# A hybrid decoder layer: gate columns in one operand, a token-major output gate, shared PSUM banks and alternating matmul widths

## Chip, cores and metric

The kernel runs on one core of one Trainium2 chip. The time is the device time of one execution in microseconds; what is compared is the median over runs.

## The reference

One layer on 256 tokens of width 2048, in float32. A token mixer (a gated delta rule of 8 heads and a pooling branch of 4 groups) shares one input projection and one output projection; a cross-attention into 256 memory tokens and a squared-ReLU MLP of width 8192 follow. The lines that matter here:

```python
proj = h @ w_in[l]                       # columns: q, k, v (3W), z (W), b (H), a (H), p
o_gdn = gated_deltanet(qkv, z, b, a, conv_w[l], a_log[l], dt_bias[l], gdn_norm_w[l])
o_pool = multiscale_pool(p, pool_w[l], pool_scale[l])
mix = jnp.concatenate([o_gdn, o_pool], axis=-1) @ w_out[l]
h = layer_norm(DEEPNORM_ALPHA * h + mix, ln1_g[l], ln1_b[l])
xa = memory_cross_attention(h, mem, xq_w[l], xk_w[l], xv_w[l], xo_w[l])
h = layer_norm(DEEPNORM_ALPHA * h + xa, ln2_g[l], ln2_b[l])
ff = jnp.square(jax.nn.relu(h @ w_up[l])) @ w_down[l]
h = layer_norm(DEEPNORM_ALPHA * h + ff, ln3_g[l], ln3_b[l])

# inside gated_deltanet
beta = jax.nn.sigmoid(b)
g = -jnp.exp(a_log) * jax.nn.softplus(a + dt_bias)
o = chunk_gated_delta_rule(q, k, v, g, beta)
o = o * lax.rsqrt(jnp.mean(o * o, axis=-1, keepdims=True) + NORM_EPS) * norm_w
o = o * jax.nn.silu(z.reshape(shp))

# inside multiscale_pool, for each of the 4 groups of 256 channels
mixed = jnp.einsum("btgc,gcd->btgd", pooled, pool_w)
return mixed.reshape(bsz, t_len, POOL_WIDTH) * pool_scale
```

## The kernel before, in words

All large products run on TensorE in a split float32: `split` (L185) writes a rounded copy of a tensor (H, the high part, ScalarE at L189) and the rest (L, the low part, VectorE at L190), both as fp32r, and a product is high times high, high times low and low times high. Weights arrive as tiles of 256 rows by 512 columns (tag W, four buffers), are split into H and L (three buffers each), and are used once. `run` (L225) walks one plan of such tiles: for tile t it issues loads, emits the splits of tiles ahead, emits the matmuls of tile t, and then lets `bg.step` (L83) emit background work (the recurrence, norms, attention) up to a budget of VectorE and ScalarE time. This order of emission is the order in which each engine executes.

Two forms of projection exist. `proj_a` (L313) keeps weights stationary and gives feature-major results. In its wide form one tile takes 8 matmuls of 512 moving columns (H against the high and low halves of the activations side by side, L328) and 8 of 256 columns (L against the high half, L332); the narrow form uses three of 256 (L349). `proj_b` (L367) keeps activations stationary and gives token-major results: one tile takes 12 matmuls of 512 columns (L374 to L376), for each of two token blocks and two row blocks in turn.

Order of the plan: w_in[0], the gate projection (`gates_plan`, L627: two tiles of 128 padded columns, of which 16 are used), w_in[1] (narrow), w_in[2] to [9] (wide; 6 and 7 are z, 8 and 9 are p), w_k 0 to 2, `pool_map(0)` (L993), w_k 3, `pool_map(1)`, w_out, w_v, w_q, w_o, and four rounds of w_up and w_down. The gates' background work (`gates`, L649) transposes the gate columns into a PSUM tile and reads it. `z_evac` (L923) folds the two halves of a wide result on ScalarE and GpSimd, and `silu` applies SiLU later; `solve` (L837) ends the recurrence and scales its output per token (L916); `gate_out` (L938) transposes each head, multiplies by norm weight and silu(z) on VectorE, and splits the result for w_out.

`pool_map` makes one 256 by 256 product for each of two groups. Each half of 128 columns (`nb`) takes 6 matmuls of 256 columns (L1003 to L1005) into a PSUM tile of its own, after which ScalarE writes the high part (L1009) and VectorE the low part (L1010), both reading PSUM. PSUM has 8 tiles of 512 columns, one bank each: four under the tag acc, which rotate, and four under aux. Waits between engines are put in by the framework from the tiles that instructions touch.

Second layer norm: `Norm.start` of token block 1 stands behind the last tile of w_o, `Norm.turn` (L1304) transposes pairs of blocks between the first up-projection tiles, and `norm1.scale(1, ALL)` (L1110 through L1336) stands behind the third of these tiles. `beside` (L1112) does the other blocks on ScalarE and GpSimd.

Of the kernel before, what the change touches and what calls it, by code (L numbers as in the profile page):

```python
# [9 lines left out]
F32 = mybir.dt.float32  # L10
F32R = mybir.dt.float32r
# [4 lines left out]
P = 128  # L16
T = 256
# [107 lines left out]
def hybrid_layer(ctx: ExitStack, tc: tile.TileContext, xT, xtok, memT, w_ba, w_in, small, w_pool,  # L125
# [99 lines left out]
    def run():  # L225
# [24 lines left out]
        def do_split():  # L250
            i = pos["split"]
            kind, src, shape, fn = plan[i][:4]
            if kind in "fwh":
# [59 lines left out]
    def proj_a(src, acts, evac, kt_outer=False, load=None, fine=0, pre=None, wide=False, spread=False):  # L313
        accs = []

        def tile_fn(k0, ns):
            def fn(h, l):
# [8 lines left out]
                def first(s, n):  # L326
                    c = slice(n * P, (n + 1) * P)
                    mm(out=accs[n], lhsT=h[:, s, c], rhs=acts[k0 + s].wide, start=k0 + s == 0, stop=False)  # L328

                def second(s, n):  # L330
                    c = slice(n * P, (n + 1) * P)
                    mm(out=accs[n][:, :T], lhsT=l[:, s, c], rhs=acts[k0 + s][0], start=False, stop=k0 + s == KT - 1)  # L332

                if wide:

                    for part in ([[(s, n) for s in range(ns)] for n in range(4)] if last else [order]):
                        for s, n in part:
                            first(s, n)
                        for s, n in part:
                            second(s, n)  # L340
# [26 lines left out]
    def proj_b(src, acts, evac, resident=False, pre=None, post=None):  # L367
# [12 lines left out]
        def both(j):  # L380
            def fn(h, l):
                if j == 0:
                    accs.extend(acc() for _ in range(NT))
                for t in range(NT):
                    for s in range(2):
                        one(t, 2 * j + s, h[:, s, :], l[:, s, :])
# [57 lines left out]
    nc.gpsimd.memset(m64[0:64, 64:128], 1.0)  # L444
    eps_ln = const.tile([P, 1], F32, name="eps_ln")
# [181 lines left out]
    def gates_plan():  # L627
        pb = []

        def fn(j):  # L630
            def f(h, l):
                if j == 0:
                    pb.append(acc())
                o = pb[0][:, :T]
                for s in range(8):
                    kt = 8 * j + s
                    a = xs[kt]
                    mm(out=o, lhsT=h[:, s, :], rhs=a[0], start=kt == 0, stop=False)
                    mm(out=o, lhsT=h[:, s, :], rhs=a[1], start=False, stop=False)
                    mm(out=o, lhsT=l[:, s, :], rhs=a[0], start=False, stop=kt == KT - 1)  # L640
                if j == 1:
                    ba.append(chunk([T]))
                    S.activation(out=ba[0], in_=o, func=AF.Copy)
                    bg.event("ba")
            return f
# [935 lines left out]
```

## Time and profile before

| | us |
|---|---|
| median of 3 runs | 1483.5 (1483.07 to 1484.04) |
| the profiled execution, its own time | 1483.14 |
| its span in the trace | 1481.3 |
| TensorE matmuls busy | 1472.4 (99%) |
| VectorE busy | 943.4 (64%) |
| ScalarE busy | 728.2 (49%) |
| GpSimd busy | 148.8 (10%) |

The span is the time from the first to the last instruction of the program in the trace; the execution's own time has 1.8 us more around it. A matmul's end is modelled and overlaps the next one, so the cost of a matmul is read from the distance of two starts, not from its duration. A timeline row merges equal instructions that follow each other (xN), and what stands in square brackets is the engine's idle time before it and what ended it.

### The profile page before, as it was taken

What the parts mean: (1) busy time and instruction counts of PE and PEld (TensorE: products, weight loads), DVE (VectorE), ACT (ScalarE), POOL (GpSimd) and SP (SyncE); (2) the same over time, 40 slices, a digit from 0 to 9 for tenths busy, and PEclk for the clock granted to TensorE, in tenths of its full rate; (3) what the DMA queues carried; (4) which work ended last, traced back from release to release, by engine and by line L of the source; (5) the groups of instructions that cost most, each with busy time, mean ns of one, the idle gap of its engine ahead of it and who ended that gap; (6) DMA issues with size and microseconds to landing.
All of it is one profiled execution on the core that took longest, in us unless ns stands there. A gap on an engine that the chain in (4) does not pass through costs nothing.

```text
span 1481.3 us, 21143 instructions
## 1 busy us (share of the span) xinstructions
PE 1472.4 (99%) x8050; PEld 1277.3 (86%) x8050; DVE 943.4 (64%) x1464; ACT 728.2 (49%) x1064; POOL 148.8 (10%) x191
## 2 busy tenths in 40 slices
PE   9999999999999999999999999999999999999998
PEld 9988889899888888998888888888888888888887
DVE  6778976867656755555685555566545565556557
ACT  6765555755533545453545443355344453345442
POOL 1024323700300000000130000000000000000001
PEclk9999999999999999999999999999999999999999
DMA  8556565535865555444735655555656655555562
GB/s 274 182 203 185 171 187 173 194 130 170 288 197 189 183 190 190 155 133 159 276 131 178 199 191 190 196 187 183 198 190 212 222 192 194 196 190 185 194 233 83
DMA packets 86902, 280.45 MB, mean 189 GB/s; under 512 B 13920, under 2 KB 15216, under 8 KB 86800
## 3 DMA queue, kind: packets, MB, share of 16 engines
q1 hardware_dynamic: 79072, 268.73, 54.7%
q0 software_dynamic: 2960, 9.58, 2.0%
q10 hardware_dynamic: 4768, 0.79, 0.3%
q8 instruction: 63, 1.03, 0.3%
q14 instruction: 39, 0.32, 0.1%
HBM read 276.43 MB, written 2.63 MB: 188 GB/s over the span
## 4 chain that ended last, share of the span: by engine, by line
PE 98%; DVE 1%; ACT 0%; issue 0%; DMA 0%; DVEq 0%; ACTq 0%
PE acc L328 30%; PE acc L332 15%; PE acc L374 13%; PE acc L376 13%; PE acc L375 13%; PE acc L349 5%; PE acc L411 0%; PE acc L410 0%; PE acc L409 0%; PE acc L1377 0%; PE acc L1379 0%; PE acc L1378 0%; PE aux L1224 0%; PE aux L1223 0%; PE aux L855 0%
## 5 line engine op out<-in xcount | busy, mean ns | idle before, releaser
L190 DVE TENSOR_TENSOR L<-W,H 128x1024 fp32r<-128x1024 f32 x469 | 578.1, 1234 | 462.2 <-ACT H L189 456.6
L189 ACT ACTIVATE H<-W 128x1024 fp32r<-128x1024 f32 x479 | 507.4, 1059 | 582.7 <-PE acc L376 298.7
L328 PE MATMUL acc<-c,H 128*128 128x512 f32 x1920 | 499.2, 394 | 0.0
L328 PEld LDWEIGHTS acc<-c,H 128*128 128x128 f32 x1920 | 338.3, 189 | 55.3 <-DVE c L190 0.6
L374 PE MATMUL acc<-H,c 128*128 128x512 f32 x832 | 325.2, 391 | 0.0
L376 PE MATMUL acc<-H,c 128*128 128x512 f32 x832 | 323.9, 389 | 0.0
L375 PE MATMUL acc<-L,c 128*128 128x512 f32 x832 | 323.9, 389 | 0.0
L332 PEld LDWEIGHTS acc<-c,L 128*128 128x128 f32 x1920 | 274.2, 190 | 27.2
L332 PE MATMUL acc<-c,L 128*128 128x256 f32 x1920 | 281.3, 282 | 0.0
L376 PEld LDWEIGHTS acc<-H,c 128*128 128x128 f32 x832 | 156.2, 188 | 32.6
L375 PEld LDWEIGHTS acc<-L,c 128*128 128x128 f32 x832 | 156.3, 188 | 31.7
L374 PEld LDWEIGHTS acc<-H,c 128*128 128x128 f32 x832 | 156.2, 188 | 31.7
L204 POOL TENSOR_TENSOR c<-c 128x256 f32<-128x256 f32 x60 | 49.8, 855 | 369.9 <-DVE L L190 186.6
L190 DVE TENSOR_TENSOR c<-c,c 128x256 fp32r<-128x256 f32 (+1 forms) x170 | 76.6, 503 | 11.4 <-ACT c L189 11.4
L189 ACT ACTIVATE c<-c 128x256 fp32r<-128x256 f32 (+1 forms) x170 | 66.6, 456 | 4.6 <-DMA c<-xT 4.6
L349 PE MATMUL acc<-c,H 128*128 128x256 f32 x384 | 66.7, 290 | 0.7 <-ACT H L189 0.7
L1095 POOL DMA_DIRECT2D c<-lnrow x24 | 12.9, 539 | 517.8 <-PE acc L376 345.0
L349 PEld LDWEIGHTS acc<-c,H 128*128 128x128 f32 x384 | 58.2, 198 | 1.6 <-ACT H L189 1.4
L349 PE MATMUL acc<-c,L 128*128 128x256 f32 x192 | 48.0, 289 | 0.0
L201 ACT ACTIVATE c<-acc 128x512 f32<-128x512 f32 x60 | 35.6, 599 | 18.9 <-PE acc L332 14.9
L566 DVE SCALAR_TENSOR_TENSOR c<-c,par 128x255 f32<-128x255 f32 (+2 forms) x72 | 38.2, 538 | 3.6 <-ACT c L563 1.9
L349 PEld LDWEIGHTS acc<-c,L 128*128 128x128 f32 x192 | 34.4, 197 | 0.2 <-DVE L L190 0.2
(258 smaller groups left out, 1000.8 us busy)
## 6 DMA issues: line engine op xcount, KB each, us to landing
W<-w_up SPq DMA_DIRECT2D x127, 512.0 KB, 4.2
W<-w_down SPq DMA_DIRECT2D x120, 512.0 KB, 4.3
W<-w_in SPq DMA_DIRECT2D x76, 512.0 KB, 3.4
W<-w_k SPq DMA_DIRECT2D x32, 512.0 KB, 3.4
W<-w_out SPq DMA_DIRECT2D x32, 512.0 KB, 4.3
W<-w_v SPq DMA_DIRECT2D x32, 512.0 KB, 3.3
W<-w_q SPq DMA_DIRECT2D x32, 512.0 KB, 3.3
W<-w_o SPq DMA_DIRECT2D x24, 512.0 KB, 3.5
```

The source lines that it names most:

```text
L189: S.activation(out=h, in_=src, func=AF.Copy)
L190: eng.tensor_tensor(out=l, in0=src, in1=h.bitcast(F32), op=ALU.subtract)
L201: S.activation(out=ab.rearrange("p s c -> p (s c)"), in_=o, func=AF.Copy)
L204: nc.gpsimd.tensor_tensor(out=r, in0=ab[:, 0, :], in1=ab[:, 1, :], op=ALU.add)
L328: mm(out=accs[n], lhsT=h[:, s, c], rhs=acts[k0 + s].wide, start=k0 + s == 0, stop=False)
L332: mm(out=accs[n][:, :T], lhsT=l[:, s, c], rhs=acts[k0 + s][0], start=False, stop=k0 + s == KT - 1)
L349: mm(out=accs[n][:, :T], lhsT=w[:, s, n * P:(n + 1) * P], rhs=acts[kt][x], start=kt == 0 and w is h and x == 0, stop=kt == KT - 1 and w is l)
L374: mm(out=accs[t], lhsT=a[0][:, c], rhs=h, start=kt == 0, stop=False)
L375: mm(out=accs[t], lhsT=a[0][:, c], rhs=l, start=False, stop=False)
L376: mm(out=accs[t], lhsT=a[1][:, c], rhs=h, start=False, stop=kt == KT - 1)
L566: V.scalar_tensor_tensor(out=u[:, sh:], in0=x[:, :T - sh], scalar=w[:, 3 - sh:4 - sh], in1=u[:, sh:], op0=ALU.mult, op1=ALU.add)
L1095: nc.gpsimd.dma_start(out=c, in_=lnrow[i:i + 1, g * 512:(g + 1) * 512].partition_broadcast(P))
```

## The change

The gate projection gets 16 columns. One tile holds its high and low parts side by side (32 stationary columns), and 16 matmuls of 512 columns replace 48 of 256; four small fp32 products with a matrix of two stacked identities (`twos`) add the four partial sums and put tokens on partitions, where two transposes stood. z goes through `proj_b`: SiLU is applied straight from PSUM, `solve` multiplies by it while it scales, and `gate_out` writes the two parts of the result from the transposed head with one ScalarE and one VectorE operation. `proj_b` (without `resident`) goes through a tile by operand first (H with the high, H with the low, L with the high part of the activations) and by token block second. `pool_map` puts both halves of a group into one PSUM tile. `norm1.scale(1, ALL)` moves from behind the third up tile to directly behind `norm1.start`. In the query projections 0 to 2 and in 15 of the 16 up projections (`turn=True`) every other tile runs its 256-column matmuls first, so that equal widths meet at the border of two tiles.

```diff
@@ -250,7 +250,11 @@
         def do_split():
             i = pos["split"]
             kind, src, shape, fn = plan[i][:4]
-            if kind in "fwh":
+            if kind in "wh" and shape == [KT, 16]:
+                h = wp.tile([P, KT, 32], F32R, tag="H", name=nm("H"), bufs=HB)
+                split(h[:, :, 0:16], h[:, :, 16:32], raw.pop(i), KT * 16)
+                parts[i] = (h, None)
...
@@ -323,21 +329,25 @@
                 if wide and k0 == 0:
                     order = [i for i in order if i[1] < 3] + [i for i in order if i[1] == 3]
 
-                def first(s, n):
+                def first(s, n, ends):
                     c = slice(n * P, (n + 1) * P)
-                    mm(out=accs[n], lhsT=h[:, s, c], rhs=acts[k0 + s].wide, start=k0 + s == 0, stop=False)
-
-                def second(s, n):
+                    mm(out=accs[n], lhsT=h[:, s, c], rhs=acts[k0 + s].wide, start=k0 + s == 0,
+                       stop=ends and k0 + s == KT - 1)
+
+                def second(s, n, ends):
                     c = slice(n * P, (n + 1) * P)
-                    mm(out=accs[n][:, :T], lhsT=l[:, s, c], rhs=acts[k0 + s][0], start=False, stop=k0 + s == KT - 1)
+                    mm(out=accs[n][:, :T], lhsT=l[:, s, c], rhs=acts[k0 + s][0], start=False,
+                       stop=ends and k0 + s == KT - 1)
 
                 if wide:
 
+
                     for part in ([[(s, n) for s in range(ns)] for n in range(4)] if last else [order]):
-                        for s, n in part:
-                            first(s, n)
-                        for s, n in part:
-                            second(s, n)
+                        low = turn and width[0] == "low" and k0 > 0
+                        for step in (second, first) if low else (first, second):
+                            for s, n in part:
+                                step(s, n, step is (first if low else second))
+                        width[0] = "high" if low else "low"
...
@@ -381,9 +391,17 @@
             def fn(h, l):
                 if j == 0:
                     accs.extend(acc() for _ in range(NT))
-                for t in range(NT):
-                    for s in range(2):
-                        one(t, 2 * j + s, h[:, s, :], l[:, s, :])
+                last = 2 * j + 2 == KT
+
+                for ts in [[t] for t in range(NT)] if last else [range(NT)]:
+                    for x, w in ((0, h), (1, h), (0, l)):
+                        for t in ts:
+                            for s in range(2):
+                                kt = 2 * j + s
+                                mm(out=accs[t], lhsT=acts[kt][x][:, t * P:(t + 1) * P], rhs=w[:, s, :],
+                                   start=kt == 0 and x == 0 and w is h, stop=kt == KT - 1 and w is l)
+                    if last:
+                        evac(ts[0], accs[ts[0]])
...
+    twos = const.tile([P, 16], F32, name="twos")
+    V.tensor_tensor(out=twos, in0=ident[:, 0:16], in1=ident[:, 16:32], op=ALU.add)
...
@@ -625,26 +645,15 @@
     ba = []
 
     def gates_plan():
-        pb = []
-
-        def fn(j):
-            def f(h, l):
-                if j == 0:
-                    pb.append(acc())
-                o = pb[0][:, :T]
-                for s in range(8):
-                    kt = 8 * j + s
-                    a = xs[kt]
-                    mm(out=o, lhsT=h[:, s, :], rhs=a[0], start=kt == 0, stop=False)
-                    mm(out=o, lhsT=h[:, s, :], rhs=a[1], start=False, stop=False)
-                    mm(out=o, lhsT=l[:, s, :], rhs=a[0], start=False, stop=kt == KT - 1)
-                if j == 1:
-                    ba.append(chunk([T]))
-                    S.activation(out=ba[0], in_=o, func=AF.Copy)
-                    bg.event("ba")
-            return f
-        for j in range(2):
-            add("w", w_ba[j], [8, P], fn(j))
+        def fn(hl, _):
+
+            o = acc()
+            for kt in range(KT):
+                mm(out=o[0:32, :], lhsT=hl[:, kt, :], rhs=xs[kt].wide, start=kt == 0, stop=kt == KT - 1)
+            ba.append(chunk([2, T]))
+            S.activation(out=ba[0][0:32].rearrange("p s c -> p (s c)"), in_=o[0:32, :], func=AF.Copy)
+            bg.event("ba")
+        add("w", w_ba, [KT, 16], fn)
...
@@ -654,14 +663,16 @@
         yield from free_aux()
         pt = aux()
         for a in range(NT):
-            nc.tensor.transpose(out=pt[:, a * P:(a + 1) * P], in_=ba[0][:, a * P:(a + 1) * P], identity=ident)
+            for s in range(2):
+                mm(out=pt[:, a * 16:a * 16 + 16], lhsT=ba[0][0:32, s, a * P:(a + 1) * P], rhs=twos[0:32, :],
+                   start=s == 0, stop=s == 1)
...
@@ -911,45 +922,42 @@
         r = small_tile([NT, 4])
         rsqrt(r, ms, [NT, 4])
         yield 1.2, 1.5, 0
+        while f"z{g}" not in bg.done:
+            yield 0, 0, 1
         for a in range(NT):
             for i in range(4):
-                V.tensor_scalar(out=os_[a][:, i, :], in0=os_[a][:, i, :], scalar1=r[:, a, i:i + 1],
-                                scalar2=None, op0=ALU.mult)
-                yield .2, 0, 0
+                V.scalar_tensor_tensor(out=os_[a][:, i, :], in0=os_[a][:, i, :], scalar=r[:, a, i:i + 1],
+                                       in1=four(zsil[g][a])[:, i, :], op0=ALU.mult, op1=ALU.mult)
+                yield .22, 0, 0
         og[g] = os_
 
-    zsil = [None] * 4
+    zsil = [[None] * NT for _ in range(2)]
 
     def z_evac(g):
-        def evac(n, o):
-            h = 4 * g + n
-            if h % 2 == 0:
-                zsil[h // 2] = chunk([2, T])
-            bg.urgent.append(silu(h, fold(o, zsil[h // 2][:, h % 2, :])))
+
+        def evac(t, o):
+            zsil[g][t] = chunk([512])
+            S.activation(out=zsil[g][t], in_=o, func=AF.Silu)
+            bg.charge(0, .65)
+            if t == NT - 1:
+                bg.event(f"z{g}")
         return evac
 
-    def silu(h, z):
-        yield 0, 0, 1
-        yield 0, 0, 1
-        S.activation(out=z, in_=z, func=AF.Silu)
-        bg.event(f"z{h}")
-        yield 0, .35, 0
-
     def gate_out(h):
+
         g, n = h // 4, h % 4
-        zs = zsil[h // 2][:, h % 2, :]
         yield from free_aux()
         ps = aux()
         for a in range(NT):
             nc.tensor.transpose(out=ps[:, a * P:(a + 1) * P], in_=og[g][a][:, n, :], identity=ident)
         yield 0, 0, 1
-        V.scalar_tensor_tensor(out=zs, in0=ps[:, :T], scalar=par[:, C_NW:C_NW + 1], in1=zs,
-                               op0=ALU.mult, op1=ALU.mult)
+        mix[8 + h] = m = pair()
+        sc = par[:, C_NW:C_NW + 1]
+        S.activation(out=m[0], in_=ps[:, :T], func=AF.Copy, scale=sc)
+        V.scalar_tensor_tensor(out=m[1], in0=ps[:, :T], scalar=sc, in1=m[0].bitcast(F32), op0=ALU.mult,
+                               op1=ALU.subtract)
         done()
-        yield .4, 0, 1
-        mix[8 + h] = pair()
-        split(*mix[8 + h], zs)
-        yield .35, .3, 0
+        yield .5, .4, 0
...
@@ -994,9 +1002,9 @@
 
         def fn(h, l):
             for gi in range(2):
+                ps = acc()
                 for nb in range(2):
-                    ps = acc()
-                    o = ps[:, :T]
+                    o = ps[:, nb * T:(nb + 1) * T]
                     for s in range(2):
...
-    proj_a(w_in[6], xs, z_evac(0), wide=True)
-    proj_a(w_in[7], xs, z_evac(1), wide=True)
+    proj_b(w_in[6], xs, z_evac(0))
+    proj_b(w_in[7], xs, z_evac(1))
...
-        proj_a(w_q[g], f1, q_evac, wide=g < 3, kt_outer=g == 0, pre={0: ["ln1_0", "ln1_1"]} if g == 0 else None)
+        proj_a(w_q[g], f1, q_evac, wide=g < 3, turn=True, kt_outer=g == 0, pre={0: ["ln1_0", "ln1_1"]} if g == 0 else None)
...
-        15: steps((norm1.start, 5, [half0, half1, (1, ALL)], [half0, half1], (2, 3))),
+        15: steps((norm1.start, 5, [half0, half1, (1, ALL)], [half0, half1], (2, 3)), (norm1.scale, (1, ALL))),
     }
     after_up = {
-        2: steps((norm1.turn, 0, 1), (norm1.scale, (1, ALL))),
+        2: steps((norm1.turn, 0, 1)),
...
-            proj_a(w_up[4 * qd + g], f2, u_evac, wide=True, spread=True)
+            proj_a(w_up[4 * qd + g], f2, u_evac, wide=True, spread=True, turn=True)
...
-        "w_ba": wba.reshape(2, 8, P, P).transpose(0, 2, 1, 3),
+        "w_ba": wba.reshape(KT, P, 16).transpose(1, 0, 2),
```

## Rows read from the trace of the kernel before

**Rows 1.** The page: busy time of each engine, granted clock in slices.

```profile
PE 1472.4 (99%) x8050; PEld 1277.3 (86%) x8050; DVE 943.4 (64%) x1464; ACT 728.2 (49%) x1064; POOL 148.8 (10%) x191
...
PEclk9999999999999999999999999999999999999999
```

**Rows 2.** Waits of PE: line, waited for, total us, times, longest.

```profile
PE aux L1311 <- DVE c L1110: 0.7, 1, 0.7
```

**Rows 3.** Timeline of PE, wide up projection: start us, us, engine, line.

```profile
963.41 0.40 PE L328 MATMUL acc<-c,H 128*128 128x512 f32 x1
...
969.00 2.00 PE L328 MATMUL acc<-c,H 128*128 128x512 f32 x8
...
971.79 2.00 PE L328 MATMUL acc<-c,H 128*128 128x512 f32 x8
...
985.75 0.63 PE L328 MATMUL acc<-c,H 128*128 128x512 f32 x2
```

**Rows 4.** Timeline of PE, from before to after four down projections.

```profile
1030.43 0.40 PE L374 MATMUL acc<-H,c 128*128 128x512 f32 x1
...
1117.49 0.39 PE L328 MATMUL acc<-c,H 128*128 128x512 f32 x1
```

**Rows 5.** Timeline of PE around gate projection and gate products.

```profile
30.56 0.28 PE L638 MATMUL acc<-c,H 128*128 128x256 f32 x1
...
36.32 0.40 PE L349 MATMUL acc<-c,H 128*128 128x256 f32 x2
...
39.20 0.38 PE L657 MATMUL aux<-ident,c 128*128 128x128 f32 x2
39.34 0.48 PE L349 MATMUL acc<-c,H 128*128 128x256 f32 x2
...
57.02 0.29 PE L700 MATMUL aux<-t,upper 128*128 128x16 f32 x2
57.15 0.37 PE L701 MATMUL aux<-t,ones 128*128 128x16 f32 x2
```

**Rows 6.** Timeline of PE and DVE at the second layer norm.

```profile
769.27 0.44 PE L1311 MATMUL aux<-ident,c 128*128 128x128 f32 x2 [0.75 <-DVE c L1110]
...
764.93 0.15 DVE L1121 SCALAR_TENSOR_TENSOR t<-t,t 128x1 f32<-128x1 f32 x1
...
767.79 1.42 DVE L1110 SCALAR_TENSOR_TENSOR c<-c,t,c 128x512 f32<-128x512 f32 x1
```

**Rows 7.** Timeline of DVE and ACT, two readers of one PSUM tile.

```profile
63.81 0.18 DVE L705 COPY G<-aux 128x32 f32<-128x32 f32 x1
...
64.03 0.27 ACT L710 ACTIVATE c<-aux 16x128 f32<-16x128 f32 x1 [1.39 <-DVE G L705]
```

**Rows 8.** Timeline around both calls of pool_map (PE, ACT, DVE).

```profile
347.83 0.28 PE L1003 MATMUL acc<-c,H 128*128 128x256 f32 x1
...
347.80 0.59 ACT L896 ACTIVATE c<-aux 128x512 f32<-128x512 f32 x1
...
349.23 1.57 ACT L1009 ACTIVATE c<-acc,par 128x256 fp32r<-128x256 f32 x4
...
350.51 1.65 DVE L1010 SCALAR_TENSOR_TENSOR c<-acc,par,c 128x256 fp32r<-128x256 f32 x4
...
375.06 0.28 PE L1003 MATMUL acc<-c,H 128*128 128x256 f32 x1
...
377.57 1.65 DVE L1010 SCALAR_TENSOR_TENSOR c<-acc,par,c 128x256 fp32r<-128x256 f32 x4
```

**Rows 9.** Evacuations of pool_map by line: ns min/median/max, first and last start.

```profile
L1009 ACT ACTIVATE c<-acc,par x8: 468/482/503, 349.2 to 377.4; 128x256 fp32r<-128x256 f32 x8
...
L1010 DVE SCALAR_TENSOR_TENSOR c<-acc,par,c x8: 473/474/478, 350.5 to 378.7; 128x256 fp32r<-128x256 f32 x8
```

**Rows 10.** Busy time by stretch: us, PE to POOL (instructions), granted clock, DMA.

```profile
5.00:10.40 5.40, 5.26 (x24) 5.26 (x25) 3.71 (x8) 3.23 (x8) 0.00 (x0) 1.00 0.95 321
10.40:36.00 25.60, 25.60 (x216) 25.60 (x215) 17.82 (x29) 17.40 (x31) 0.00 (x0) 1.00 0.86 288
```

More of the change, by code (lines that the diff above doesn't have):

```diff
@@ L252, in do_split @@
             kind, src, shape, fn = plan[i][:4]
-            if kind in "fwh":
+            if kind in "wh" and shape == [KT, 16]:
+                h = wp.tile([P, KT, 32], F32R, tag="H", name=nm("H"), bufs=HB)
+                split(h[:, :, 0:16], h[:, :, 16:32], raw.pop(i), KT * 16)
+                parts[i] = (h, None)
+            elif kind in "fwh":
                 h = wp.tile([P] + shape, F32R, tag="H", name=nm("H"), bufs=HB)
@@ L310, in add, with proj_a @@
         plan.append((kind, src, shape, fn, pre, post))
-    def proj_a(src, acts, evac, kt_outer=False, load=None, fine=0, pre=None, wide=False, spread=False):
+    width = ["low"]
+    def proj_a(src, acts, evac, kt_outer=False, load=None, fine=0, pre=None, wide=False, spread=False, turn=False):
         accs = []
@@ L656, in gates @@
         for a in range(NT):
-            nc.tensor.transpose(out=pt[:, a * P:(a + 1) * P], in_=ba[0][:, a * P:(a + 1) * P], identity=ident)
+            for s in range(2):
+                mm(out=pt[:, a * 16:a * 16 + 16], lhsT=ba[0][0:32, s, a * P:(a + 1) * P], rhs=twos[0:32, :],
+                   start=s == 0, stop=s == 1)
         yield 0, .2, 1
-        ptv = pt[:, :T].rearrange("p (a c) -> p a c", a=NT)
+        ptv = pt[:, :2 * 16].rearrange("p (a c) -> p a c", a=NT)
         e = small_tile(sh)
@@ L663, in gates @@
         u = small_tile(sh)
-        V.tensor_tensor(out=u, in0=ptv[:, :, 32:40],
+        V.tensor_tensor(out=u, in0=ptv[:, :, 8:16],
                         in1=par[:, C_DT:C_DT + 8].unsqueeze(1).to_broadcast([P, NT, HEADS]), op=ALU.add)
@@ L1029, in hybrid_layer @@
     for h in range(HEADS):
-        bg.add(f"gate{h}", gate_out(h), f"solve{h // 4}", f"z{h}")
+        bg.add(f"gate{h}", gate_out(h), f"solve{h // 4}")
     for h in range(HEADS):
@@ L1540, in _layout @@
     b, a, p = wi[:, 4096:4104], wi[:, 4104:4112], wi[:, 4112:]
-    wba = np.zeros((D, P), wi.dtype)
-    wba[:, 0:8] = b
-    wba[:, 32:40] = a
+    wba = np.concatenate([b, a], axis=1)
     cw = f(conv_w)[0].reshape(4, 3, 8, P)[:, [1, 0, 2]]
```

## The prediction

> **What bounds the kernel now.** I read the page first: TensorE is busy 99% of the span, at full granted clock in all 40 slices, and no other engine passes 64% [rows 1]. So only two things can move the time: how fast matmuls follow each other, and stretches in which TensorE waits. I then read the waits of TensorE; the one that the change touches is 0.7 us in the second layer norm, and it is the longest that stands between the kernel's first and last microseconds [rows 2]. Last I read start-to-start distances in the timeline, since durations overlap. A down projection of `proj_b` has 96 matmuls of 512 columns; four of them take 1117.49 - 1030.43 = 87.06 us, so 21.77 us each and 0.2267 us a matmul [rows 4]. A wide projection (64 matmuls of 512 and 64 of 256 columns) takes 985.75 - 963.41 = 22.34 us [rows 3]. The gate projection's 48 matmuls of 256 columns take 36.32 - 30.56 = 5.76 us, 0.120 us each [rows 5].
>
> **Gate projection.** 48 x 0.120 = 5.76 us becomes 16 matmuls of 512 columns: 16 x 0.2267 = 3.63 us, so -2.13 us. No row shows 32 stationary columns; I take the price of 128, since the moving columns carry it. The two transposes (39.20 to 39.34, 0.14 us for two) become four fp32 products of 16 columns; one such product is two instructions, 57.02 to 57.15, 0.14 us [rows 5], so 0.55 us, and +0.4 net (bounds +0.1 to +0.8). Net -1.7 us, all on TensorE, which waits for nothing there. The 0.9 MB less of DMA, one weight split less, the `twos` sum (VectorE idle ahead of the first load) and one slot less in the plan cost nothing: background work follows the gate event, which moves with its tile.
>
> **z through proj_b.** Two wide projections of 22.34 us become two of 21.77 us: -1.15 us. SiLU from PSUM, the product inside `solve` and the shorter `gate_out` lie on ScalarE, VectorE and GpSimd and replace more work than they bring; TensorE's continuous work covers them. The cover would be gone if the gated heads came late at the fifth tile of w_out, and they come one slot earlier than now.
>
> **Order inside proj_b.** Same 12 matmuls per tile at the same 0.2267 us; L is asked for later, which no wait of before needed. Nothing, on either side.
>
> **Alternating widths.** One wide tile takes 971.79 - 969.00 = 2.79 us [rows 3], against 8 x (0.2267 + 0.120) = 2.77 us without a change of width: 0.02 us for a pair of changes. Over a projection it is 22.34 - 64 x 0.3467 = 0.15 us. Eleven pairs (7 tiles, 4 parts of the last) become six, so I take half: 0.07 us, times 18 projections, -1.2 us. Bounds: 0 (the price is in the first matmuls after the change, and may stay) and -2.7 us (all of it goes); a loss would need an L that is not there yet, and splits run two tiles ahead.
>
> **Layer norm.** TensorE waits 0.75 us for a VectorE scaling that was emitted late (767.79) and took 1.42 us [rows 6]. Emitted behind `norm1.start` it runs at 765.1, right after that step's last small operation (764.93), and even at 1.42 us it is done before the transposes' turn at 768.5 (769.27 less the 0.75 waited). -0.8 us; the next transposes want blocks that GpSimd has finished by then.
>
> These sum to -1.7 - 1.15 - 1.2 - 0.8 = -4.85 us.
>
> **pool_map.** This is the part that I think decides. Both halves of a group now lie in one PSUM tile, and between them stand the two evacuations of the first half. Does the second half's first matmul wait for these, though it writes other columns? The trace of before has no such write, but it has two readers of one PSUM tile that share no column: `gates` reads columns 0 to 31 of `pg` on VectorE (L705) and columns 128 to 255 on ScalarE (L710). ScalarE sits idle 1.39 us and starts 0.04 us after VectorE is done; the profile names L705 as what it waited for [rows 7]. They share nothing but the tile. So waits go by PSUM tile, not by column, and I take it that a matmul is held too. The Trainium skill says the same of the chip: in "PSUM — Partial Sum Buffer", section "PSUM bank collisions raise a hardware error", engines have to be kept apart by bank and partition quadrant, not by address, TensorE's writes included; by that rule the halves must take turns and the sum below is +3.65 us, where waits by column would make it -4.85; the row agrees with the page.
>
> The price. At the first call the second half starts at 347.83 now, and the first half's evacuations run only later: ScalarE has recurrence work (347.80) and a weight split ahead of L1009 (349.23), VectorE a weight split ahead of L1010, which starts at 350.51 [rows 8] and takes 0.47 us [rows 9]. TensorE resumes at about 351.05: 3.2 us lost; 2.6 us if that one piece of recurrence work (0.59 us) falls elsewhere. I take 2.9. At the second call: 377.57 + 0.47 + 0.06 against 375.06, so 3.0 us [rows 8]. In each call the second group's wait finds both queues empty: 0.28 us to the last matmul's end, 0.48 us ScalarE, 0.47 us VectorE [rows 9], some 0.15 us for three handovers (0.04 each in rows 7), less the 0.12 us that passes anyway: 1.3 us. Four waits: 2.9 + 3.0 + 1.3 + 1.3 = 8.5 us. Bounds: 0 if a matmul is not held, 5.2 (four times 1.3), 8.8. TensorE is the bound on both sides of the calls, so a wait there is not given back. In return, w_out finds fresh tiles, but TensorE does not wait there now.
>
> **Sum.** -4.85 + 8.5 = +3.65 us. The profiled execution took 1483.14 us (span 1481.3 and 1.8 around it), so 1486.8; the median of runs lies 0.4 above it, so 1487.2 us forecast.
>
> **Rivals.** (a) *A matmul is not held*: waits by column, for writes at least. Then 1483.5 - 4.85 = 1478.7 us, faster; it decides from whether the first L1003 of a second half follows the last L1005 at 0.12 us. Against it stand rows 7; for it only that no row shows a write. (b) *The waits are short*: the queues are empty at both calls since background work has moved; 4 x 1.3 = 5.2 us, so 1483.9 us, no change. Against it: the weight split ahead of the evacuations belongs to the plan, not to the background. (c) *The clock falls*: TensorE stands some 3 us, then works 1.4 us, then stands again. In the first 5.4 us of the kernel 24 matmuls of 256 columns filled 5.26 us (0.21 us each, 1.2 GHz), then 216 filled 25.6 us (0.12, 2.4 GHz), though the granted clock reads 1.00 in both [rows 10]. That start lost 24 x 0.09 = 2.3 us; as much after each call gives 1487.2 + 4.6 = 1491.8, after one 1489.5. Mid-kernel gaps of before end at 0.75 us [rows 2, 6], so nothing shows where this begins. The Trainium skill has it in "TensorE: Matmul & The Clock Gate", section "HAM oscillation — how this bites in real kernels": matmul bursts with gaps between them can return to half rate; no run shown here has that.
>
> **How the numbers follow.** Forecast 0.58, (b) 0.20, (c) 0.13, (a) 0.09. A measurement of this kernel tells 0.2%, 3 us, from no change. Of the forecast's 0.58 about 0.48 lies over +3 us and 0.10 under it; (c) is all slower; (b) 0.18 same and 0.02 slower; (a) faster. So faster 0.09, same 0.28, slower 0.63. The forecast's own range is 1485.5 to 1489 (its terms' bounds); with (b) at 1483.9 and the milder (c) at 1489.5 the range is 1483.0 to 1490.0, which leaves out (a) and the harder (c).
>
> **What would show it.** In the trace after: waits of PE at L1003 on VectorE's L1010 (line numbers shift), four, two near 3 us and two near 1.3 us; the gate projection in 3.6 us; z projections of 21.8 us; wide up projections of 22.27 us; no wait of the second norm's transposes. The prediction is wrong if the second halves follow at 0.12 us, if a new wait shows at the first p tile (its third and fourth PSUM tiles are those that SiLU empties last) or at w_out, or if matmuls after the calls run at 0.21 us.

## The result and the profile after

The changed kernel takes 1492.1 us (median; runs from 1490.2 to 1496.3) where the kernel before takes 1483.3 in the same measurement: a ratio of 1.0063, 95% interval 1.0052 to 1.0074. It is slower, as forecast, but by 8.8 us and not by 3.7, and the time lies 2.1 us above the top of the range. The profiled execution of after is its longest one, 1496.3 us with a span of 1494.6 us, so the stages below are compared with that time: 13.2 us above the 1483.14 of before.

The page of after, busy time by engine and the granted clock in 40 slices, against [rows 1]:

```profile
PE 1477.6 (99%) x7960; PEld 1277.6 (85%) x7960; DVE 953.7 (64%) x1454; ACT 719.4 (48%) x1049; POOL 141.5 (9%) x185
...
PEclk9999999998899999999999999999999999999999
```

TensorE is as busy as before by share, with fewer matmuls, yet two slices have lost granted clock. Both lie at `pool_map`. The waits of TensorE in after (tile, line, releaser: us in total, times, longest us), against [rows 2]:

```profile
PE acc L1011 <- DVE c L1018: 7.9, 4, 3.1
...
PE acc L401 <- DVE L L190: 0.4, 1, 0.4
PE aux L857 <- DVE c L889: 0.4, 1, 0.4
PE aux L866 <- DVE c L860: 0.2, 1, 0.2
```

The 0.7 us of the layer norm is gone. The largest wait of the kernel is new: four waits of the first matmul of a second half (L1011, L1003 before) for VectorE's low part (L1018, L1010 before), 7.9 us idle. The timeline of TensorE around the first call (start, duration, engine, line, shapes, and in brackets the idle time and its releaser), against [rows 8]:

```profile
348.08 0.28 PE L1013 MATMUL acc<-c,L 128*128 128x256 f32 x1
351.51 0.58 PE L1011 MATMUL acc<-c,H 128*128 128x256 f32 x1 [3.15 <-DVE c L1018]
351.89 0.41 PE L1012 MATMUL acc<-c,H 128*128 128x256 f32 x1
352.11 0.41 PE L1013 MATMUL acc<-c,L 128*128 128x256 f32 x1
...
354.02 0.41 PE L1013 MATMUL acc<-c,L 128*128 128x256 f32 x1
355.52 0.58 PE L1011 MATMUL acc<-c,H 128*128 128x256 f32 x1 [1.08 <-DVE c L1018]
```

From the last matmul of one half to the first of the next, 351.51 - 348.08 = 3.43 us pass where 0.12 would do: 3.31 lost. The other three lose 1.38 (355.52 - 354.02 = 1.50), 2.73 and 1.38: 8.80 us in all. What the first wait is made of stands on ScalarE and VectorE (same columns):

```profile
348.57 0.21 ACT L502 ACTIVATE t<-t 128x8 f32<-128x8 f32 x1 [0.29 <-DVE t L921]
348.69 1.04 ACT L189 ACTIVATE H<-W 128x1024 fp32r<-128x1024 f32 x1
349.63 0.45 ACT L1017 ACTIVATE c<-acc,par 128x256 fp32r<-128x256 f32 x1
...
349.83 1.23 DVE L190 TENSOR_TENSOR L<-W,H 128x1024 fp32r<-128x1024 f32 x1
350.98 0.48 DVE L1018 SCALAR_TENSOR_TENSOR c<-acc,par,c 128x256 fp32r<-128x256 f32 x1
```

A weight split stands ahead of the evacuation on either engine, as the prediction read it from before: VectorE starts L1018 at 350.98 (L1010 started at 350.51 before) and TensorE goes on 0.05 us after it ends.

The second thing is in the timeline of TensorE above: behind the wait, matmuls of 256 columns start 0.22 us apart (352.11 - 351.89) where 0.12 is their distance at full clock [rows 5]. The granted clock says so too. Windows of after (stretch, length, then busy us and instructions of PE, PEld, DVE, ACT, POOL, granted clock, DMA share, GB/s):

```profile
350.70:361.00 10.30, 8.40 (x29) 7.34 (x30) 5.00 (x12) 3.97 (x9) 2.71 (x6) 0.50 0.76 252
361.00:384.80 23.80, 21.89 (x133) 19.30 (x131) 13.34 (x20) 12.68 (x18) 3.99 (x7) 1.00 0.54 177
384.84:395.08 10.24, 8.53 (x28) 7.37 (x29) 4.48 (x10) 4.09 (x9) 2.97 (x6) 0.50 0.82 261
```

Two stretches of some 10.2 us run at 1.2 GHz, each from inside the first wait of a call to behind it, and between them TensorE is back at 2.4. Half of the 8.40 + 8.53 us that TensorE worked there is time lost, 8.5 us by this. The stages give a little less: from the first z projection's start to the second w_out projection's, after takes 16.4 us more than before (258.86 against 242.42). The version below that has neither the waits nor the lower clock (tiles of its own, and the evacuations ahead of a weight split) takes 242.41 us there, so all other terms cancel. The four waits are 8.8, and some 7.6 are left for the clock.

Stage by stage, from the start of one stage's first matmul to the next one's, us:

| stage | before | after | difference |
|---|---|---|---|
| gate projection | 5.76 | 3.69 | -2.07 |
| w_in[1], with the four small products | 24.42 | 25.07 | +0.65 |
| first and second z projection | 22.34 / 25.73 | 22.47 / 26.28 | +0.13 / +0.55 |
| `pool_map(0)` with the background work behind it | 4.80 | 9.49 | +4.69 |
| w_k 3 | 22.43 | 25.04 | +2.61 |
| `pool_map(1)` with the background work behind it | 3.75 | 8.92 | +5.17 |
| first w_out projection | 21.90 | 23.75 | +1.85 |
| first up projection (layer norm in it) | 25.67 | 24.74 | -0.93 |
| a later up projection | 22.34 | 22.30 | -0.04 |

The two `pool_map` rows carry less background work than before: 16 matmul instructions of `solve` (eight products of two each) and 2 transposes of `gate_out` stood behind the first call and 8 transposes behind the second; in after none do, they ran earlier. That matters below.

### The profile page after: what moved, and what is told of

Read it like the earlier page. It is cut to its first block, busy times and chain, and to the rows that moved or that the text cites. A ratio compares the mean times of both kernels' runs of the same rounds, so it can differ in the third digit from the quotient of the medians.

```text
span 1494.6 us, 20937 instructions
## 1 busy us (share of the span) xinstructions
PE 1477.6 (99%) x7960; PEld 1277.6 (85%) x7960; DVE 953.7 (64%) x1454; ACT 719.4 (48%) x1049; POOL 141.5 (9%) x185
## 4 chain that ended last, share of the span: by engine, by line
PE 97%; DVE 2%; ACT 0%; issue 0%; DMA 0%; DVEq 0%; ACTq 0%
PE acc L401 40%; PE acc L334 27%; PE acc L339 14%; PE acc L359 5%; DVE L L190 1%; PE acc L429 1%; PE acc L427 1%; PE acc L428 1%; PE acc L1385 1%; PE acc L1387 0%; PE acc L1386 0%; PE acc L385 0%; PE acc L386 0%; PE acc L384 0%; ACT H L189 0%
## 5 line engine op out<-in xcount | busy, mean ns | idle before, releaser
L334 PE MATMUL acc<-c,H 128*128 128x512 f32 x1792 | 451.5, 394 | 0.1
L401 PE MATMUL acc<-H,c 128*128 128x512 f32 x1792 | 451.0, 391 | 0.0
L401 PEld LDWEIGHTS acc<-H,c 128*128 128x128 f32 x1792 | 335.5, 188 | 68.7
L334 PEld LDWEIGHTS acc<-c,H 128*128 128x128 f32 x1792 | 323.1, 189 | 57.6 <-DVE c L190 0.5
L339 PEld LDWEIGHTS acc<-c,L 128*128 128x128 f32 x1792 | 244.6, 191 | 18.0
L339 PE MATMUL acc<-c,L 128*128 128x256 f32 x1792 | 249.9, 282 | 0.0
L401 PE MATMUL acc<-L,c 128*128 128x512 f32 x896 | 244.6, 390 | 0.4 <-DVE L L190 0.4
L401 PEld LDWEIGHTS acc<-L,c 128*128 128x128 f32 x896 | 168.5, 188 | 36.1 <-DVE L L190 0.8
L359 PEld LDWEIGHTS acc<-c,H 128*128 128x128 f32 x384 | 58.0, 197 | 2.0 <-ACT H L189 1.6
L359 PE MATMUL acc<-c,L 128*128 128x256 f32 x192 | 47.4, 286 | 0.0
L190 POOL TENSOR_TENSOR L<-W,H 128x1024 fp32r<-128x1024 f32 x12 | 30.5, 2542 | 105.2 <-ACT H L189 105.2
L218 ACT ACTIVATE c<-acc 128x256 f32<-128x256 f32 x60 | 23.0, 384 | 23.3 <-PE acc L334 13.8
L359 PEld LDWEIGHTS acc<-c,L 128*128 128x128 f32 x192 | 34.0, 194 | 0.0
```

The source lines that it names most:

```text
L190: eng.tensor_tensor(out=l, in0=src, in1=h.bitcast(F32), op=ALU.subtract)
L218: S.activation(out=r, in_=o[:, :T], func=AF.Copy)
L359: mm(out=accs[n][:, :T], lhsT=w[:, s, n * P:(n + 1) * P], rhs=acts[kt][x], start=kt == 0 and w is h and x == 0, stop=kt == KT - 1 and w is l)
L401: mm(out=accs[t], lhsT=acts[kt][x][:, t * P:(t + 1) * P], rhs=w[:, s, :], start=kt == 0 and x == 0 and w is h, stop=kt == KT - 1 and w is l)
```

## Experiments

### The shared tile taken back

Everything else of the change stays; each half has its own PSUM tile again.

```diff
-                ps = acc()
                 for nb in range(2):
-                    o = ps[:, nb * T:(nb + 1) * T]
+                    ps = acc()
+                    o = ps[:, :T]
```

> The changed kernel with a PSUM tile of its own for each half in pool_map, as before; all other edits stay. Theory (waits): the four waits on the evacuations (8.8 us in the start-to-start distances) and the half-clock stretches behind them go, and what the other edits gave in the two traces stays (start of the kernel -1.8, layer norm -0.9, alternating widths -0.7, z and solve about +0.2): 1480 us, granted clock 1.00. Rival (another edit, z through proj_b above all, brings the loss or the clock's fall): 1487 us or more, or a clock of 0.5 somewhere in mid-kernel.

Measured: 1481.9 us (10 runs, 1480.0 to 1482.7), ratio to before 0.9996 (0.9987 to 1.0005), with the granted clock at 1.00 throughout the profile. So 10.2 us of after hang on the shared tile, the four waits and the lower clock together. But without it the change is worth 1.2 us by the medians, not 4.85, and the interval includes no change; the time is 1.9 us above what was expected of this kernel. Waits of TensorE in this kernel:

```profile
PE acc L334 <- DVE c L1018: 1.0, 1, 1.0
...
PE acc L401 <- DVE c L1018: 0.4, 1, 0.4
PE acc L401 <- DVE L L190: 0.4, 1, 0.4
```

Two of these are new: the first tile of w_k 3 (L334) and of w_out (L401) wait for the evacuations of `pool_map`. In before those had cover, the background products behind the calls; in this kernel the recurrence is done earlier, and nothing stands between `pool_map` and the next projection.

### The shared tile alone

The kernel before, with the same edit in `pool_map` made and nothing else.

```diff
+                ps = acc()
                 for nb in range(2):
-                    ps = acc()
-                    o = ps[:, :T]
+                    o = ps[:, nb * T:(nb + 1) * T]
```

> The kernel before with one edit: both halves of a group of pool_map in one PSUM tile. Theory (waits): four waits of the second half on VectorE, two near 3 us and two near 1.3 us, +8 to +9 us, and a half-clock stretch behind none, one or both calls, another 3 to 4 us each: 1491.5 to 1499 us. Rival (the waits came from the changed order of the other work): under 1488 us.

Measured: 1496.5 us (1495.5 to 1497.8), ratio 1.0096 (1.0081 to 1.0111): the edit by itself costs 13.4 us. Its waits and its stretches of lower clock:

```profile
PE acc L1003 <- DVE c L1010: 8.1, 4, 3.1
```

```profile
349.72:356.55 6.83, 5.75 (x28) 5.45 (x27) 2.25 (x6) 2.74 (x6) 0.00 (x0) 0.50 0.24 77
383.86:390.69 6.83, 5.75 (x27) 5.45 (x26) 1.65 (x4) 2.60 (x6) 3.75 (x8) 0.50 0.95 313
```

The same four waits, and a fall of the clock at both calls (6.8 us each here), so neither needs any other part of the change.

### Same shared tile, both halves written ahead of the evacuations

All 12 matmuls of a group come first, then the four evacuations. The tile is shared, but nothing reads it between the writes of its halves.

```diff
                         mm(out=o, lhsT=l[:, gi, s, c], rhs=a[0], start=False, stop=s == 1)
+                for nb in range(2):
+                    o = ps[:, nb * T:(nb + 1) * T]
                     b = 4 * g + 2 * gi + nb
```

> The changed kernel, still one PSUM tile for both halves, but all 12 matmuls of a group are issued ahead of the four evacuations of that group. Theory (waits): sharing a tile costs nothing when nothing is read between the two writes: no wait in pool_map, 1480 us, as with tiles of their own. Rival (the shared tile itself costs, through its slower release or through the product's own start): 1483 us or more.

Measured: 1483.7 us (1482.0 to 1484.9), ratio 1.0004 (0.9995 to 1.0014). No wait is left inside `pool_map`: TensorE is held by readers that stand between the writes, and sharing alone does not hold it there. The time is a miss, 3.7 us above what was expected and 1.8 above the kernel with tiles of its own. The rival, 1483 us or more through a slower release of the tile, had the number, and the trace shows its mechanism. Waits, a window, and the evacuations behind the first high part in this kernel:

```profile
PE acc L334 <- DVE c L1020: 1.8, 2, 1.1
```

```profile
355.46:358.86 3.40, 3.40 (x12) 2.92 (x12) 3.40 (x7) 1.56 (x3) 0.00 (x0) 0.50 0.95 283
```

```profile
352.01 0.84 ACT L1019 ACTIVATE c<-acc,par 128x256 fp32r<-128x256 f32 x2 [1.42 <-DVE c L1020]
...
351.50 0.48 DVE L1020 SCALAR_TENSOR_TENSOR c<-acc,par,c 128x256 fp32r<-128x256 f32 x1
352.51 0.88 DVE L1020 SCALAR_TENSOR_TENSOR c<-acc,par,c 128x256 fp32r<-128x256 f32 x2 [0.54 <-ACT c L1019]
353.93 0.48 DVE L1020 SCALAR_TENSOR_TENSOR c<-acc,par,c 128x256 fp32r<-128x256 f32 x1 [0.54 <-ACT c L1019]
```

And VectorE's four low parts at the same call in the kernel with tiles of its own:

```profile
350.81 1.65 DVE L1018 SCALAR_TENSOR_TENSOR c<-acc,par,c 128x256 fp32r<-128x256 f32 x4
```

In both kernels the first low part starts 3.5 us after the call's first matmul (347.98 here, 347.30 there). With tiles of its own the four take 1.65 us. Over shared tiles they take 2.91 (351.50 to 354.41), since the two readers of a tile take turns: ScalarE's high part of a second half waits for VectorE's low part of the first. So the tiles come free later, and the first tile of w_k 3 waits twice, 1.10 and 0.68 us. Behind these two the clock is at half for 3.4 us, which costs 1.7.

### The gap filled

After, with matmuls that nobody reads, into a third tile, between the halves: 6 in the first group of a call, 2 in the second. The waits for the evacuations stay as they are; only what TensorE does in them differs.

```diff
                 for nb in range(2):
+                    if nb:
+                        fill = acc()
+                        for _ in range(6 if gi == 0 else 2):
+                            mm(out=fill[:, :T], lhsT=warm[:, :P], rhs=warm[:, :T], start=True, stop=True)
```

> The changed kernel with matmuls that nobody reads (float32, 256 columns of zeros, into a third PSUM tile) between the halves: 6 in the first group and 2 in the second, some 2.6 and 0.9 us, a little less than the waits. The halves still wait for the evacuations. Theory (the idle time of TensorE lowers the clock): no stretch at half clock in any run, so about 1490 us in all runs, the level of the changed kernel's runs with a mean clock of 0.999. Rival (the clock falls for another reason, such as the load of the other stages): half-clock stretches stay and runs reach 1494 to 1496 us.

Measured: 1488.3 us (1487.2 to 1489.7), ratio 1.0040 (1.0025 to 1.0055), 3.8 us less than after though it issues more matmuls. The two calls with what follows them:

```profile
346.00:362.00 16.00, 15.22 (x89) 13.00 (x89) 12.17 (x30) 8.94 (x17) 6.23 (x11) 1.00 0.79 256
380.00:396.00 16.00, 15.78 (x78) 12.88 (x77) 8.69 (x14) 7.73 (x12) 2.93 (x6) 1.00 0.86 278
```

The clock stays at 2.4 GHz through both, in all four runs of this kernel. So it is the idle time of TensorE that brought the clock down, not the sharing itself. Without the fall the waits cost about what the prediction gave them: 1488.3 is 6.4 us above the kernel with tiles of its own, which has 1.4 us of waits that a shared tile doesn't have, so 7.8.

### After once more

The changed kernel, unchanged, beside the kernels below.

> The changed kernel once more, beside the variants of this set. It was 1490.2 to 1496.3 us at mean clocks of 0.999 to 0.993; the theory (four waits, then a half-clock stretch behind none, one or both calls of pool_map) expects the runs to stand in levels by mean clock again: near 1490 at 0.999, near 1494 at 0.995 to 0.996, near 1496 at 0.993.

Measured: 1492.2 us (1488.6, 1492.1, 1492.3, 1496.1), ratio 1.0063 (1.0047 to 1.0079). The profile is of the 1488.6 execution. Its waits, and its only stretch at half clock:

```profile
PE acc L1011 <- DVE c L1018: 7.9, 4, 3.1
```

```profile
349.60:353.00 3.40, 2.88 (x12) 2.63 (x12) 0.95 (x3) 0.48 (x1) 2.42 (x5) 0.50 0.77 222
353.02:1486.00 1132.98, 1123.37 (x5835) 962.37 (x5834) 675.15 (x924) 514.51 (x716) 38.98 (x53) 1.00 0.58 189
```

The waits are the same to a tenth; the stretch at half clock is 3.4 us and not two of 10.2. TensorE worked 2.88 us in it against 16.93 in the other profile; half of the difference is 7.0, and the executions differ by 1496.3 - 1488.6 = 7.7 us. So the spread of this kernel's runs is the clock's: over both measurements, executions with a mean granted clock of 0.999 took 1488.6 to 1490.5 us, those with 0.995 to 0.997 took 1492.1 to 1494.0, those with 0.993 took 1496.1 and 1496.3.

### One wait for each call

The loops of `pool_map` swapped: the first halves of both groups, then the second halves, over two shared tiles.

```diff
-            for gi in range(2):
-                ps = acc()
-                for nb in range(2):
+            two = [acc() for _ in range(2)]
+            for nb in range(2):
+                for gi in range(2):
+                    ps = two[gi]
```

> The changed kernel with the same two shared PSUM tiles in pool_map, filled in another order: first halves of both groups, then second halves. Between the two halves of a tile stand 6 more matmuls, and the second tile's evacuations follow the first's at once. Theory (waits by tile): one wait a call instead of two, some 2.4 and 1.9 us long, so 4.3 us instead of 7.9: 1486.5 us without a half-clock stretch, up to 1492.5 with one behind each call. Rival (the shared tile holds TensorE until the whole tile is released): both waits stay, 1490 us or more.

Measured: 1487.2 us (1484.5 to 1488.6), ratio 1.0026 (1.0015 to 1.0037). One wait is left for each call, as the number of reader-to-writer turns demands:

```profile
PE acc L1012 <- DVE c L1019: 4.3, 2, 2.4
```

```profile
352.50:355.91 3.41, 3.41 (x15) 3.22 (x16) 0.89 (x3) 1.24 (x3) 1.73 (x4) 0.50 0.82 251
383.22:386.63 3.41, 3.41 (x12) 2.83 (x11) 2.04 (x3) 2.85 (x7) 1.21 (x3) 0.50 1.00 310
```

A single gap, 2.44 us at the first call and 1.85 at the second, already brings the clock down, for 3.4 us a call, 1.7 us each. At the second call the half rate begins 1.2 us after TensorE has gone on (383.22 against 382.07).

### Tiles of its own, and the evacuations ahead of a weight split

The kernel with tiles of its own left two waits on the evacuations of `pool_map`, each with the split of a later weight tile queued ahead of it. Here that one split is emitted behind the evacuations.

```diff
-            while pos["split"] < n and (held[0] < HB or pos["split"] <= t
+            while pos["split"] < n and (held[0] < HB - (shape == [2, 2, 256]) or pos["split"] <= t
```

> The changed kernel with PSUM tiles of their own in pool_map, as in the first experiment, and with the weight split of a later tile emitted behind the evacuations of pool_map instead of ahead of them. In the first experiment TensorE waited 1.0 us at the first tile of w_k 3 and 0.4 us at w_out for these evacuations. Theory (they are late because a split of 1.06 us ScalarE and 1.23 us VectorE is queued ahead of them): both waits go, 1480.4 us against 1481.9. Rival (they are late because of the folds of the projection ahead): the waits stay and the time is 1481.9 us or, with the split now late for its own tile, more.

Measured: 1480.0 us (1478.1 to 1480.5, 11 runs), ratio 0.9977 (0.9968 to 0.9986). Both waits are gone, and TensorE goes from `pool_map` into w_k 3 without a gap. VectorE at the first call, this kernel:

```profile
349.71 0.17 DVE L513 TENSOR_TENSOR t<-t,t 128x8 f32<-128x8 f32 x1
349.79 1.73 DVE L1018 SCALAR_TENSOR_TENSOR c<-acc,par,c 128x256 fp32r<-128x256 f32 x4
```

The four low parts run in one go from 349.79, where a split of 1.23 us came first. This version beats both kernels.

### z through `proj_b`, alone

The kernel before with the z part only: `proj_b` in its old order, SiLU from PSUM, the product in `solve`, the shorter `gate_out`.

```diff
-    proj_a(w_in[6], xs, z_evac(0), wide=True)
-    proj_a(w_in[7], xs, z_evac(1), wide=True)
+    proj_b(w_in[6], xs, z_evac(0))
+    proj_b(w_in[7], xs, z_evac(1))
...
```

> The kernel before with z alone through proj_b (SiLU from PSUM, the product in solve, the shorter gate_out); the matmul order inside proj_b stays as before. Prediction's theory: both z projections take 0.58 us less, start to start, than before. Rival (a weight split is late there): TensorE waits for VectorE's low part, now the second operand asked for, by 0.5 us or more, and the gain is gone.

Measured: 1484.0 us in its one execution, 1483.3 before. The two projections did get shorter by 0.54 and 0.53 us (22.34 to 21.80 and 25.73 to 25.20), close to the 0.58 costed, and no split is late in them. It came back as waits:

```profile
PE aux L855 <- DVE c L849: 1.1, 1, 1.1
PE acc L328 <- DVE c L1007: 0.9, 1, 0.9
PE acc L374 <- DVE c L1007: 0.8, 1, 0.8
```

The first, in `solve`, was 0.3 before. The other two are w_k 3 and w_out on the evacuations of `pool_map`: moving z changes where the recurrence's products fall, and by itself it takes away their cover. Where the 16 instructions of `solve` stood behind the first call, TensorE now goes from the last matmul of `pool_map` straight to the wait:

```profile
350.75 0.28 PE L1002 MATMUL acc<-c,L 128*128 128x256 f32 x1
351.94 2.12 PE L328 MATMUL acc<-c,H 128*128 128x512 f32 x8 [0.91 <-DVE c L1007]
```

### The best version without its z part

The version with the evacuations ahead, z back in `proj_a` with its folds, `silu` and the longer `gate_out`.

```diff
-    proj_b(w_in[6], xs, z_evac(0))
-    proj_b(w_in[7], xs, z_evac(1))
+    proj_a(w_in[6], xs, z_evac(0), wide=True)
+    proj_a(w_in[7], xs, z_evac(1), wide=True)
...
```

> The variant with tiles of their own and the evacuations ahead of the split (1480.0 us), with z put back to what it was before: wide projections, fold and SiLU apart, the old gate_out. Theory (z through proj_b saves 1.15 us of matmul time but gives it back in waits of the recurrence and one late weight split, as that variant's trace shows by stage): 1480.0 us, no difference beyond 0.5 us. Rival (z is a net gain as the prediction had it): 1481.2 us.

Measured: 1481.5 us (1479.2 to 1482.9), ratio 0.9989 (0.9980 to 0.9998) against 0.9977 with z. Its new wait is for a fold on ScalarE:

```profile
PE acc L334 <- ACT c L201: 1.1, 1, 1.1
```

So z is worth some 1.5 us among the other edits, where no difference was expected; the two intervals overlap, so the size is less sure than the sign. It is not what z saves over before: with the same z as before, this kernel takes 2.3 us more than before from the start of z to the second w_out projection (244.69 against 242.42), 1.1 of it the wait above, at the first p projection, which before does not have. Nor are the products of `solve` behind the first `pool_map` here (w_k 3 starts 2.88 us after the call's first matmul), so z is not the only edit that moves them.

### The best version with the old order in `proj_b`

```diff
-                for ts in [[t] for t in range(NT)] if last else [range(NT)]:
-                    for x, w in ((0, h), (1, h), (0, l)):
...
+                for t in range(NT):
+                    for s in range(2):
+                        one(t, 2 * j + s, h[:, s, :], l[:, s, :])
```

> The variant with tiles of their own and the evacuations ahead of the split (1480.0 us), with the matmul order inside proj_b of before (operands innermost, token blocks outside). Prediction's theory: no difference, 1480.0 us, since the matmuls are the same at the same distance. Rival (the low part asked for last is what keeps a wait away in the z stage or at w_out): 1480.5 us or more, with a longer wait of TensorE on VectorE's low part in the first z projection.

Measured: 1481.4 us (1479.2 to 1482.5), ratio 0.9987 (0.9979 to 0.9996). The first z projection takes 23.33 us where it takes 22.36 with the new order, and the wait is in the list:

```profile
PE acc L385 <- DVE L L190: 1.2, 1, 1.2
```

No difference had been the theory; the rival, a longer wait for a low part, is what came. With the new order the same split (161.68, for 1.21 us) is done before its low part is asked for at 163.18, and no wait stands at that tile, the third; the 0.3 us of that kernel is at the seventh. The order that asks for L last gains some 0.9 us. Alone, z through `proj_b` in the old order met no such wait; which of the other edits makes that split late was not tried.

## Why the prediction was right, and where it was wrong

**The halves take turns: right.** The step that carried the sign, a matmul that waits for readers of other columns of its PSUM tile, was argued from two readers [rows 7]; the traces show it for a write, four times, and the kernel that reads nothing between the writes has no such wait. The rule from the Trainium skill that the prediction weighed ("PSUM — Partial Sum Buffer", section "PSUM bank collisions raise a hardware error") points the same way, and the trace agrees; the runs can't tell whether the chip or only the framework's waits demand it.

**The price of the waits: right, in part by luck.** 8.5 us forecast, 8.80 measured: 2.9 against 3.31, 3.0 against 2.73, twice 1.3 against twice 1.38. The first was the middle of 2.6 and 3.2, the lower end for the case that one piece of recurrence work (L896 on ScalarE) leaves the queue. It did leave, but other recurrence work came in its place: ScalarE's split followed a small operation at 348.57 (L502) that had waited for VectorE, and started at 348.69; before, the same split followed L896:

```profile
348.28 1.06 ACT L189 ACTIVATE H<-W 128x1024 fp32r<-128x1024 f32 x1
```

So the upper end came about in another way than was argued. That the weight split stands ahead of the evacuation was read rightly.

**The clock: the step that failed.** The forecast let the matmuls behind the waits run at 0.120 us. They ran at 0.21, one of the signs of being wrong that the prediction named. The kernel with the gaps filled shows what this alone does: with the clock held it takes 1488.3 us, 1.1 above the forecast and inside its range; with the fall the time is 1492.1. The clock had its place as rival (c), with 0.13, and its higher price, two falls, 1491.8 us, is 0.3 us from the median. That closeness is partly luck: its savings of 4.85 us were some 1.5 too large (below), and its clock term, 4.6, was 0.8 above the 3.8 that filling the gaps gave back. Two things were wrong in it. The chance: no gap of before above 0.75 us stands in mid-kernel, so the trace held nothing against a fall, yet it was given less than the rival of short waits, which the rows spoke against. Hence the range stopped at 1490.0. And the price: 2.3 us a fall was read from the kernel's start [rows 10] (the row gives 5.26 - 24 x 0.12 = 2.4); behind the waits it was between 1.4 us (2.88 busy at half clock) and 4.3 (8.53), whichever way the execution went. "TensorE: Matmul & The Clock Gate" in the Trainium skill, section "HAM oscillation — how this bites in real kernels", says that idle gaps between bursts of matmuls bring the half rate back. The traces agree, with 0.50 granted behind gaps of 3.15 us in after, and of 2.44 and 1.85 us in the kernel with one wait a call.

**The savings: mis-sized, and one of them was paid with cover.** Forecast -4.85 us; the kernel with tiles of its own shows -1.2 by the medians (interval -1.9 to +0.7), and the best version, without its two waits, -3.3.

- The gate projection gave 2.07 us (forecast 2.13), and the small products cost 0.65 where 0.4 was taken: -1.4 for -1.7. The four products, eight instructions, take 37.88 - 36.89 = 0.99 us, 0.25 each where the nearest row had given 0.14 [rows 5]. Lines of the timeline of after:

```profile
30.22 0.40 PE L652 MATMUL acc<-c,H 128*32 128x512 f32 x1
33.92 0.28 PE L359 MATMUL acc<-c,H 128*128 128x256 f32 x1
...
36.89 1.06 PE L667 MATMUL aux<-twos,c 32*128 32x16 f32 x8
37.88 0.50 PE L359 MATMUL acc<-c,H 128*128 128x256 f32 x2
```

- The layer norm gave 0.93 (forecast 0.8), and its wait is gone.
- Alternating widths gave 0.04 us a projection, not 0.07: 999.35 - 977.05 = 22.30 us from the first matmul of one up projection to that of the next in after, against 22.34 [rows 3]. Not every projection gained as much: the 15 up projections and the three query projections together are 0.7 us shorter, for 1.2 forecast. No run isolates this edit.

```profile
977.05 0.40 PE L334 MATMUL acc<-c,H 128*128 128x512 f32 x1
...
999.35 0.40 PE L334 MATMUL acc<-c,H 128*128 128x512 f32 x1
```

- z gave its 0.54 and 0.53 us of matmul time where it stood alone. The step "TensorE's continuous work covers them" counted z's own operations but not what follows when the recurrence's products fall elsewhere: they had covered `pool_map`'s evacuations. That is 1.0 + 0.4 us of new waits with tiles of its own, and 0.4 for a late L. From the start of z to the second w_out projection that kernel takes 2.0 us more than before, and the best version as much as before. The kernel without the z part shows that the other edits move the products as well.
- "Nothing" for the order inside `proj_b` looked only at waits of before. In the changed kernel an L does come late, and the order is worth about 1.4 us by the medians, 0.9 by the waits.
- "w_out finds fresh tiles, but TensorE does not wait there now" was true of before and not of after: the other edits make that wait. The shared tile then pays 10.2 us to be rid of 1.4; emitting one split later removes them and gains 1.9 us by the medians.

**What stays open.** Why one and the same wait is followed by 3.4, 6.8 or 10.2 us at half clock. Which edits besides z move the recurrence's products away from `pool_map`, and how. And the time of z alone, 0.7 us above before, comes from one execution, no more than the measurement can tell.

## What to carry to other kernels

Two results in one PSUM tile are one resource for every reader and writer: give each its own tile where there is room. Putting no evacuation between their writes spares TensorE the waits there, but the readers still take turns, which cost 1.8 us here, the lower clock behind the two waits included. On an engine that is always busy, price a new wait at its length and add half of the matmul time behind it that may run at half clock; such a wait doesn't end where the trace shows the engine starting again. Before moving background work, list which waits it covers now, and look at what is queued ahead of the evacuations on the engine that frees the tile.

## What was not expected of the hardware

The clock fell in or behind gaps shorter than the 2.8 us of one wide weight tile: 2.44 and 1.85 us in the kernel with one wait a call, 1.10 and 0.68 us close together in the kernel with late evacuations. Inside the first gap of after it had fallen by 350.70, before TensorE went on at 351.51. The stretches at 1.2 GHz lasted 3.4, 6.8 or 10.2 us, differing between executions of the same kernel with the same waits, so a kernel with such gaps has a wide spread of times: 1488.6 to 1496.3 us for after, 1478.1 to 1480.5 for the version without them. Unread matmuls in the gap held the clock at 2.4 GHz and gave back 3.8 us. And two engines that read different columns of one PSUM tile took turns, which stretched four evacuations from 1.65 to 2.91 us.
